# Gate products as a task of their own on DVE, full and begun output tiles in turn, small weights loaded two ahead, in a two-layer hybrid decoder trunk

## The chip, the cores and the metric

One core of one Trainium2 chip runs the whole trunk. The time is device microseconds of one execution; the median of the runs counts. TensorE (PE) makes matrix products into PSUM, VectorE (DVE), ScalarE (ACT) and GpSimd (POOL) work on tiles of 128 partitions, and SyncE (SP) issues nearly all transfers in one queue. Each engine works its queue in order.

## What is computed

Two pre-norm residual layers over 512 positions of width 2048. One input projection feeds four groups of heads (latent attention, a diagonal state-space layer, RWKV-7, differential attention) and a gate; the four outputs, concatenated, are multiplied by SiLU of the gate and projected back. Cut from the reference:

```python
def rms_norm(x, g, eps=NORM_EPS):
    xf = x.astype(jnp.float32)
    y = xf * lax.rsqrt(jnp.mean(xf * xf, axis=-1, keepdims=True) + eps)
    return (y * g.astype(jnp.float32)).astype(x.dtype)
# each layer: h = rms_norm(x); z = h @ w_in, its columns shared out among the branches;
# y = concat(mla, s5, rwkv7, diff);  x = x + (y * silu(gate)) @ w_out;  after the last layer rms_norm
```

All is float32. The weights of the large projections are 2048 x 6656 (padded) and 2048 x 2048 for each layer.

## The kernel before

All activations are kept transposed, features on partitions, as tiles of 128 x 512. Every float32 product is made of three products in a rounded format: an operand is split into a rounded high part (`wh`, `XH`, `MH`, by ACT) and the rest (`wl`, `XL`, `ML`, by DVE). `three` issues the three matmuls.

`big` is the stream that fills PE: for an output tile it walks 16 blocks of 128 inputs in pieces of four. `weights` loads a piece (`raw`, 256 KB, SP), ACT makes `wh` and DVE makes `wl`, with three buffers each (`ring`), so raw piece j waits until split j-3 is made, and the splits run up to three pieces ahead of PE. They have priority AHEAD in the compiler's scheduler, which otherwise orders ACT, DVE, POOL and SP by its own estimate of time. PE's order is written out by hand: `Clock` counts PE's time as issued products, and tasks (`spawn`) give work between two fill products when their pause, the number that they yield, is over. `late` ties an instruction behind the newest AHEAD split on its engine.

`in_proj` runs the 52 tiles of ORDER, the gate last. `evacuate` takes each tile out of PSUM on DVE; of a gate tile it makes twice SiLU in a tile `stg` (`zd` on ACT between) and, where the matching branch output is ready, goes on to `mix` at once, else stores it to DRAM (`gD`). `mix` loads the branch output `yD` into `zr`, of which there is one buffer, multiplies on POOL (L1462), and makes `MH` on ACT (L1463) and `ML` on DVE (L1464). `mix_one` fetches a stored gate tile and mixes it; `mixing` calls it at every fourth fill product.

When the first 12 gate products exist, `partial` begins output tiles over 12 of the 16 blocks, in the order of PART, and stores them as `xP`, until the other tasks are done. `out_proj` then goes through the 16 output tiles from 0 to 15: begun ones need one piece, the others four. Each is added to the residual on DVE (`xo`, L1545) and, in layer 0, given to `absorb`, which makes `XH` and `XL` of the next layer and the sum of squares (`sum_sq`: ACT squares, POOL adds, L471). The S5 tables of layer 1 (`s5_tables`) are made on DVE, ACT and POOL at the same time, with a pause of 4.5 between steps. In layer 1 `last_proj` does the same, with the final norm.

`small` does the small products of the branches (w_glu, w_uk, w_uq) with one raw buffer, the next weights loaded while one is in use.

Of the kernel before, what the change touches and what calls it, by code (L numbers as in the profile page):

```python
# [187 lines left out]
def trunk(ctx, tc, io, KT=16, depth=DEPTH):  # L188
# [45 lines left out]

    def weights(pl, src, n, bufs, first=0, into=None):

        w = WCOL
        with tc.high_priority(offset=first) if first else ExitStack():
            raw = pl.tile([128, w], F32, tag="raw", name="raw", bufs=bufs[0])
            SP.dma_start(out=raw[:, :n], in_=src)  # L240
            wh, wl = into or (pl.tile([128, w], F32R, tag=t, name=t, bufs=bufs[1]) for t in ("wh", "wl"))
            x = A.copy(out=wh[:, :n], in_=raw[:, :n])  # L242
            y = V.tensor_sub(out=wl[:, :n], in0=raw[:, :n], in1=wh[:, :n])  # L243
# [35 lines left out]
    def small(pl, srcs, nk, rh, rl, done, bufs=(1, 2)):  # L279

        nxt = weights(pl, srcs[0], nk * 128, bufs)
        for j in range(len(srcs)):
            wh, wl = nxt
            if j + 1 < len(srcs):
                nxt = weights(pl, srcs[j + 1], nk * 128, bufs)
# [53 lines left out]
    def s5_tables(pl, l, pace):  # L339
# [76 lines left out]
        for q in range(4):  # L416
# [38 lines left out]
            SP.dma_start(out=s5tab[l, q], in_=cs2.rearrange("p a g q -> p a (g q)"))  # L455


    def absorb(sp, k, x, pvt, sqs, eng=G):
# [434 lines left out]
    def s5_glu(gp, l, P, uD, ysD, out):  # L893
# [42 lines left out]
        yield from small(gp, [io["w_glu"][l, t] for t in range(4)], 4, GH, GL, done)  # L936
# [32 lines left out]
    def low_rank_col(pl, sqs, n, rxc, name, mul):  # L969
# [3 lines left out]
        yield 9.0  # L973
# [11 lines left out]
    def load_split(pl, src, n, P, g, name):  # L985
# [12 lines left out]
        for t in range(n):  # L998
# [9 lines left out]
            if t + 2 < n:  # L1008
                rs.append(load(t + 2))
                yield 4.0  # L1010
        return xh, xl, sqs

    def mla_kv(pa, l, P, aD, rxc, knD, vtD):
        def at():
            return pa.tile([128, S], F32, name="at", tag="at", bufs=3)

        kh, kl, ksq = yield from load_split(pa, aD[0:2], 2, P, "kvg", "ck")
# [9 lines left out]
        yield from small(pa, [io["w_uk"][l, h] for h in range(4)], 2, kh, kl, done)  # L1027
        ws = [weights(pa, io["w_uv"][l, :, k * 512:k * 512 + 512], 512, (1, 2)) for k in range(2)]
# [10 lines left out]
    def mla_q(pa, l, P, aD, rxc, qnD, qrD):  # L1039
        qh, ql, sqs = yield from load_split(pa, aD[3:7], 4, P, "qg", "cq")  # L1040
# [3 lines left out]
        order = (4, 5, 0, 1, 2, 3)  # L1044
# [7 lines left out]
        yield from small(pa, [io["w_uq"][l, j] for j in order], 4, qh, ql, done)  # L1052
# [258 lines left out]
    def tables(l):  # L1311
        with sub("tab", l) as st:
            yield from s5_tables(st, l, 3.0 if l == 0 else 4.5)
        PE.done.add((l, "tab"))

    class Layer:
        def __init__(self, l):
# [8 lines left out]
            self.MH, self.early, self.part, self.mixed = None, [], [], set()  # L1326
# [89 lines left out]
        def evacuate(self, n, t, ps):  # L1416
# [27 lines left out]
            else:  # L1444
# [341 lines left out]
```

## Time and profile before

| | |
|---|---|
| median of three runs | 2024.81 us (2019.72 to 2025.67) |
| the profiled execution | 2023.16 us |
| its span in the trace | 2021.4 us |
| mean granted clock of PE | 0.982 |
| PE, DVE, ACT, POOL busy | 1955.9, 1303.5, 831.8, 368.4 us |

The profile tells for each engine the time in which it was busy, what ended its idle time (the releaser), and in stretches of time what each did. PE stands at 2.4 GHz where the granted clock is 1.00 and at 1.2 GHz where it is 0.50. Matmuls are pipelined: a row's duration overlaps its neighbours', so a rate is read from the starts or from a group of them.

### The profile page before, as it was taken

What the parts mean: (1) busy time and instruction counts of PE and PEld (TensorE: products, weight loads), DVE (VectorE), ACT (ScalarE), POOL (GpSimd) and SP (SyncE); (2) the same over time, 40 slices, a digit from 0 to 9 for tenths busy, and PEclk for the clock granted to TensorE, in tenths of its full rate; (3) what the DMA queues carried; (4) which work ended last, traced back from release to release, by engine and by line L of the source; (5) the groups of instructions that cost most, each with busy time, mean ns of one, the idle gap of its engine ahead of it and who ended that gap; (6) DMA issues with size and microseconds to landing.
All of it is one profiled execution on the core that took longest, in us unless ns stands there. A gap on an engine that the chain in (4) does not pass through costs nothing.

```text
span 2021.4 us, 31452 instructions
## 1 busy us (share of the span) xinstructions
PE 1955.9 (97%) x10975; PEld 1596.9 (79%) x10975; DVE 1303.5 (64%) x2801; ACT 831.8 (41%) x1734; POOL 368.4 (18%) x422
## 2 busy tenths in 40 slices
PE   9979999999999999998999999999999998999997
PEld 7767877788888787886788888778787787887787
DVE  6886866546776577649646686664683675766442
ACT  5543434344234355434433233443332353554351
POOL 1112203123001122004101111312210112200122
PEclk9989989999999999998999999999999999999998
DMA  5453545455462455455642445365456437445553
GB/s 209 142 167 117 144 119 148 155 169 171 151 214 95 146 179 172 154 171 179 203 133 93 136 119 155 96 194 170 160 158 172 150 100 224 131 145 167 159 175 116
DMA packets 241422, 311.08 MB, mean 154 GB/s; under 512 B 83312, under 2 KB 109168, under 8 KB 241264
## 3 DMA queue, kind: packets, MB, share of 16 engines
q1 hardware_dynamic: 241120, 308.91, 49.3%
q8 instruction: 86, 1.41, 0.3%
q14 instruction: 72, 0.59, 0.1%
q10 hardware_dynamic: 144, 0.17, 0.0%
HBM read 235.75 MB, written 70.88 MB: 152 GB/s over the span
## 4 chain that ended last, share of the span: by engine, by line
PE 77%; DMA 8%; DVE 7%; ACT 3%; issue 2%; POOL 1%; SPq 1%; DVEq 0%; POOLq 0%; ACTq 0%
PE acc L126 57%; PE pb L126 18%; PE pb L130 2%; DVE wl L243 1%; DMA zr<-yD 1%; POOL stg L1462 1%; DMA raw<-in_w_out_dram 1%; DMA raw<-qkD 1%; ACT K L850 1%; DMA raw<-in_w_in_dram 1%; DMA T<-K 1%; DMA qs<-qrD 0%; SPq L854 0%; DMA xo<-xP 0%; DMA gD<-stg 0%
## 5 line engine op out<-in xcount | busy, mean ns | idle before, releaser
L126 PE MATMUL acc<-XH,wl 128*128 128x512 f32 x1600 | 654.8, 409 | 20.3 <-DVE zr L504 10.7
L126 PE MATMUL acc<-XL,wh 128*128 128x512 f32 x1600 | 629.9, 394 | 1.1 <-DVE XL L463 1.1
L126 PE MATMUL acc<-XH,wh 128*128 128x512 f32 x1600 | 629.9, 394 | 0.0
L242 ACT CAST wh<-raw 128x512 fp32r<-128x512 f32 (+1 forms) x560 | 342.4, 616 | 563.9 <-PE acc L126 415.9
L243 DVE TENSOR_TENSOR wl<-raw,wh 128x512 fp32r<-128x512 f32 (+1 forms) x560 | 395.3, 710 | 257.5 <-ACT wh L242 253.1
L126 PEld LDWEIGHTS acc<-XH,wl 128*128 128x128 f32 x1600 | 303.8, 190 | 95.2 <-DVE zr L504 11.2
L126 PEld LDWEIGHTS acc<-XH,wh 128*128 128x128 f32 x1600 | 303.1, 189 | 66.0
L126 PEld LDWEIGHTS acc<-XL,wh 128*128 128x128 f32 x1600 | 304.1, 190 | 60.7 <-DVE XL L463 2.7
L126 PE MATMUL acc<-MH,wl 128*128 128x512 f32 x448 | 180.9, 404 | 12.5 <-DVE xo L1545 10.1
L126 PE MATMUL acc<-ML,wh 128*128 128x512 f32 x448 | 176.5, 394 | 0.2 <-DVE ML L1464 0.2
L126 PE MATMUL acc<-MH,wh 128*128 128x512 f32 x448 | 176.5, 394 | 0.0
L703 POOL TENSOR_SCALAR tmp<-SV,ec 64x64 f32<-64x64 f32 x112 | 69.8, 625 | 339.8 <-DVE SV L730 171.7
L126 PEld LDWEIGHTS acc<-MH,wl 128*128 128x128 f32 x448 | 85.3, 190 | 32.7 <-DVE xo L1545 11.8
L126 PEld LDWEIGHTS acc<-MH,wh 128*128 128x128 f32 x448 | 85.0, 190 | 18.3
L126 PEld LDWEIGHTS acc<-ML,wh 128*128 128x128 f32 x448 | 85.3, 190 | 16.5 <-DVE ML L1464 0.5
L1462 POOL TENSOR_TENSOR stg<-stg,zr 128x512 f32<-128x512 f32 x32 | 45.7, 1428 | 178.3 <-DMA zr<-yD 67.4
L471 POOL TENSOR_TENSOR sqs<-sqs,sq 128x512 f32<-128x512 f32 (+1 forms) x32 | 42.3, 1321 | 133.6 <-ACT sq L469 133.5
L1279 POOL TENSOR_TENSOR sr<-ss,cc 128x1 f32<-128x1 f32 x32 | 21.8, 686 | 188.0 <-DVE ss L1277 178.2
L955 ACT ACTIVATE pt<-pb,nb,fc 128x128 f32<-128x128 f32 (+3 forms) x64 | 39.5, 618 | 32.9 <-DVE nb L954 32.5
L640 DVE TENSOR_TENSOR tmp<-X 64x30 f32<-64x30 f32 (+14 forms) x120 | 39.2, 326 | 11.0 <-DMA X<-nD 5.1
L953 DVE TENSOR_REDUCE mx<-pb 128x1 f32<-128x128 f32 (+3 forms) x96 | 45.9, 478 | 0.5
L1463 ACT ACTIVATE MH<-stg 128x512 fp32r<-128x512 f32 x32 | 20.1, 631 | 57.3 <-POOL stg L1462 50.5
(398 smaller groups left out, 2908.6 us busy)
## 6 DMA issues: line engine op xcount, KB each, us to landing
raw<-in_w_in_dram SPq DMA_DIRECT2D x416, 256.0 KB, 3.4
raw<-in_w_out_dram SPq DMA_DIRECT2D x128, 256.0 KB, 3.4
zr<-yD SPq DMA_DIRECT2D x32, 256.0 KB, 2.9
gD<-stg SPq DMA_DIRECT2D x22, 256.0 KB, 3.3
stg<-gD SPq DMA_DIRECT2D x22, 256.0 KB, 3.4
zD<-stg SPq DMA_DIRECT2D x18, 256.0 KB, 3.1
xP<-stg SPq DMA_DIRECT2D x18, 256.0 KB, 2.1
xo<-xP SPq DMA_DIRECT2D x18, 256.0 KB, 3.4
```

Of the source, the lines that this page charges most:

```text
L126: return self.nc.tensor.matmul(out, lhsT=lhsT, rhs=rhs, **kw)
L130: return self.nc.tensor.transpose(out, in_, identity)
L242: x = A.copy(out=wh[:, :n], in_=raw[:, :n])
L243: y = V.tensor_sub(out=wl[:, :n], in0=raw[:, :n], in1=wh[:, :n])
L471: eng.tensor_tensor(out=sqs, in0=sqs, in1=sq, op=ALU.add)
L640: i = V.tensor_tensor(out=t2, in0=X[:, 0:j, j:j + 1].to_broadcast([64, j, n]), in1=X[:, j:j + 1, j + 1:32].to_broadcast([64, j, n]), op=AL ...
L703: G.tensor_scalar(out=T1[T, h], in0=SVs[s][T, c, h], scalar1=ec[T, h, c:c + 1], scalar2=None, op0=ALU.mult)
L850: A.copy(out=K[:, g], in_=ps[32 * g:32 * g + 16, 0:128])
L953: V.tensor_reduce(out=mx, in_=ps[:, 0:n], axis=AX.X, op=ALU.max)
L955: A.activation(out=pt, in_=ps[:, 0:n], func=AF.Exp, scale=fcol[:, qb:qb + 1], bias=nb, accum_out=sm)
L1279: G.tensor_tensor(out=sr, in0=ss, in1=C("mhalf", 0, 1), op=ALU.pow)
L1462: G.tensor_tensor(out=g, in0=g, in1=y, op=ALU.mult)
```

## The change

A gate product is no longer made where the gate tile is. Every gate tile goes to DRAM; a task `mixer` (one for each layer, spawned with `in_proj`) takes tiles whose gate and branch output exist, loads both into one of two pairs of buffers (`zr` with `w2a2`, `y` with `lo`; the last three names are of tiles that are free by then), and a pause later issues the product on DVE, then `MH` and `ML`. `mix`, `open_mix`, `mix_one` and `mixing` are gone. `partial` stops when all 16 products exist. `out_proj` puts the begun tiles between the others. `sum_sq` adds on DVE. `weights` is cut in two, and `small` and w_uv load two pieces ahead, split with `late`. Some pauses and buffer counts are changed.

```diff
-    def small(pl, srcs, nk, rh, rl, done, bufs=(1, 2)):
-        nxt = weights(pl, srcs[0], nk * 128, bufs)
+    def small(pl, srcs, nk, rh, rl, done, raws):
+        def split(j):
+            wh, wl, x, y = split_w(pl, raws[j], nk * 128, 2)
+            late(x)
+            if j + 2 < len(srcs):
+                raws.append(load_w(pl, srcs[j + 2], nk * 128, 2))
+            return wh, wl
+        nxt = split(0)
...
-    def sum_sq(lp, sqs, src, first, eng=G):
+    def sum_sq(lp, sqs, src, first, bufs=2):
...
-            eng.tensor_tensor(out=sqs, in0=sqs, in1=sq, op=ALU.add)
+            V.tensor_tensor(out=sqs, in0=sqs, in1=sq, op=ALU.add)
...
-        yield 9.0
+        yield 6.0
...
-                yield 4.0
+                yield 3.0
...
-            t = pd.tile([128, S], F32, name="raw", tag="raw", bufs=3)
+            t = pd.tile([128, S], F32, name="raw", tag="raw", bufs=4)
...
                 r = raw(kpD)
+                load(0)
                 yield Y["ld"]
                 hd["kp"] = split("kp", r)
-                load(0)
-                yield Y["ld"]
...
-            yield from s5_tables(st, l, 3.0 if l == 0 else 4.5)
+            yield from s5_tables(st, l, 2.5 if l == 0 else 3.0)
...
-                if self.MH is not None and (l, "y", t) in PE.done:
-                    self.mix(t, g)
-                else:
-                    SP.dma_start(out=self.gD[t], in_=g)
-                    self.early.append(t)
+                SP.dma_start(out=self.gD[t], in_=g)
+                self.gates.append(t)
...
-            G.tensor_tensor(out=g, in0=g, in1=y, op=ALU.mult)
-            A.mul(out=self.MH[:, t], in_=g, mul=0.5)
...
+        def mixer(self, mctx):
+            l, on, n = self.l, [], 0
+            yield from self.need(("rwkv",))
...
+            while len(self.mixed) < 16:
+                t = next((t for t in self.gates if (l, "y", t) in PE.done), None)
+                if t is not None and len(on) < 2:
+                    self.gates.remove(t)
+                    (a, x), (b, z) = (((zp, "zr"), (cp, "w2a2")), ((mp, "y"), (cp, "lo")))[n % 2]
+                    y, g = (q.tile([128, S], F32, name=w, tag=w, bufs=1) for q, w in ((a, x), (b, z)))
+                    SP.dma_start(out=y, in_=self.yD[t])
+                    SP.dma_start(out=g, in_=self.gD[t])
+                    on.append((PE.t + Y["ld"], t, y, g))
+                    n += 1
+                elif on and on[0][0] <= PE.t:
+                    _, t, y, g = on.pop(0)
+                    late(V.tensor_tensor(out=g, in0=g, in1=y, op=ALU.mult))
+                    A.mul(out=self.MH[:, t], in_=g, mul=0.5)
...
+                yield 1.5
...
-                if (l, "others") in PE.done:
+                if len(self.mixed) == 16:
                     break
...
-            for m in range(KT):
+            order, rest = [], [m for m in range(KT) if m not in self.part]
+            for j, m in enumerate(rest):
+                order += [m] + self.part[j * len(self.part) // len(rest):(j + 1) * len(self.part) // len(rest)]
+            for m in order:
```

In SP's queue, in the gate stretch of layer 1, before (`zr` is the branch output, `stg` the gate tile, `raw<-in_w_in` a weight piece, `qkD` and `vD` the attention's tiles):

```order
L1483 DMA stg<-gD_10476 128x512
L1227 DMA raw<-qkD_10467 64x512
L1461 DMA zr<-yD_10464 128x512
L240 DMA raw<-in_w_in_dram 128x512
L1207 DMA raw<-vD_10468 128x512
L1483 DMA stg<-gD_10476 128x512
L1208 DMA raw<-qkD_10467 128x512
L1461 DMA zr<-yD_10464 128x512
L240 DMA raw<-in_w_in_dram 128x512 x2
```

and after, where the two pairs take turns:

```order
L1498 DMA w2a_17465<-gD_10493 128x512
L237 DMA raw<-in_w_in_dram 128x512 x2
L1497 DMA y<-yD_10481 128x512
L1498 DMA lo<-gD_10493 128x512
L237 DMA raw<-in_w_in_dram 128x512 x2
L1497 DMA zr<-yD_10481 128x512
L1479 DMA gD_10493<-stg 128x512
L1498 DMA w2a_17602<-gD_10493 128x512
L237 DMA raw<-in_w_in_dram 128x512 x2
```

Both loads of a product now stand together, with two weight pieces between one pair and the next.

In DVE's queue, in the same stretch, before there is `ML` alone (`pb`, `mx`, `nb` are steps of a softmax):

```order
L243 TENSOR_TENSOR wl<-raw,wh 128x512
L1449 TENSOR_TENSOR stg<-acc,rxr 128x512
L1451 SCALAR_TENSOR_TENSOR stg<-zd,stg 128x512
L243 TENSOR_TENSOR wl<-raw,wh 128x512
L1464 SCALAR_TENSOR_TENSOR ML<-stg,MH 128x512
L952 TENSOR_TENSOR pb<-pb,cc 128x128 x3
```

and after:

```order
L244 TENSOR_TENSOR wl<-raw,wh 128x512
L1503 TENSOR_TENSOR lo<-lo,y 128x512
L974 RECIPROCAL ri<-sme 128x1
L1292 TENSOR_TENSOR ri<-ri,nl 128x1
L1293 SCALAR_TENSOR_TENSOR pt<-pt,ri 128x384
L1505 SCALAR_TENSOR_TENSOR ML<-lo,MH 128x512
L1304 TENSOR_SCALAR ss<-ss 128x1
L1309 TENSOR_SCALAR on<-pb,sr 128x128
L244 TENSOR_TENSOR wl<-raw,wh 128x512
```

The product stands right behind a weight split, and its `ML` ahead of the next one.

In DVE's queue, among the output tiles of layer 0, before (`st...` and `s5par` are steps of the tables):

```order
L1545 TENSOR_TENSOR xo<-acc,xo 128x512
L410 TENSOR_SCALAR sthi<-sth 128x32
L243 TENSOR_TENSOR wl<-raw,wh 128x512
L463 SCALAR_TENSOR_TENSOR XL<-xo,pvt,XH 128x512
L310 TENSOR_SCALAR scs<-scs 128x32
```

and after:

```order
L244 TENSOR_TENSOR wl<-raw,wh 128x512
L1564 TENSOR_TENSOR xo<-acc,xo 128x512
L468 TENSOR_SCALAR cs_9814<-cs_9814,cc 128x512
L458 TENSOR_TENSOR tq<-cc,sthi 128x512
L468 TENSOR_SCALAR cs_9952<-cs_9952,cc 128x512
L244 TENSOR_TENSOR wl<-raw,wh 128x512
L458 TENSOR_TENSOR tq<-cc,sthi 128x512
L459 TENSOR_SCALAR tr<-tq 128x512
L1564 TENSOR_TENSOR xo<-acc,xo 128x512
L325 TENSOR_SCALAR cs_9814<-cs_9814 128x512
L479 SCALAR_TENSOR_TENSOR XL<-xo,pvt,XH 128x512
L459 TENSOR_SCALAR tr<-tq 128x512
L487 TENSOR_TENSOR sqs<-sqs,sq 128x512
```

The add of squares (L487) has joined each tile's work on DVE.

## Rows read from the trace of the kernel before

**Rows 1.** Page, part 1: busy us (share of the span) x instructions, each engine.
```profile
PE 1955.9 (97%) x10975; PEld 1596.9 (79%) x10975; DVE 1303.5 (64%) x2801; ACT 831.8 (41%) x1734; POOL 368.4 (18%) x422
```

**Rows 2.** Waits of PE, releaser named: us in total, times, longest.
```profile
PE acc L126 <- DVE zr L504: 10.7, 1, 10.7
PE acc L126 <- DVE xo L1545: 10.1, 4, 4.6
PE pb L126 <- ACT PT L965: 7.9, 4, 4.3
...
PE acc L126 <- DVE stg L1449: 5.2, 2, 4.9
```

**Rows 3.** Stretches: length; PE, PEld, DVE, ACT, POOL busy; clock; DMA share; GB/s.
```profile
450.00:500.00 50.00, 50.00 (x255) 40.50 (x254) 34.72 (x49) 21.67 (x38) 14.62 (x12) 1.00 0.53 174
...
750.00:800.00 50.00, 45.02 (x209) 36.72 (x208) 39.04 (x88) 26.47 (x62) 16.13 (x13) 0.93 0.56 174
```

**Rows 4.** Timeline, gate products of layer 1: SP, POOL, ACT, PE in turn.
```profile
1710.49 0.32 SPq L1461 DMA_DIRECT2D zr<-yD  x1
...
1713.45 1.75 POOL L1462 TENSOR_TENSOR stg<-stg,zr 128x512 f32<-128x512 f32 x1 [3.00 <-DMA zr<-yD]
...
1715.23 0.63 ACT L1463 ACTIVATE MH<-stg 128x512 fp32r<-128x512 f32 x1 [1.96 <-POOL stg L1462]
...
1717.37 0.80 PE L126 MATMUL acc<-XH,wl 128*128 128x512 f32 x1 [4.93 <-DVE stg L1449]
```

**Rows 5.** Chain of work, an undisturbed stretch of PE: start, us, count.
```profile
971.69 59.48 PE acc L126 x261
```

**Rows 6.** Timeline of PE: other waits of the gate stretches.
```profile
766.16 1.23 PE L126 MATMUL pb<-dVT,PT 128*128 128x128 f32 x4 [4.26 <-ACT PT L965]
...
1698.05 0.50 PE L126 MATMUL acc<-XH,wl 128*128 128x512 f32 x1 [1.57 <-DVE wl L243]
...
1912.27 0.49 PE L126 MATMUL acc<-MH,wl 128*128 128x512 f32 x1 [1.20 <-ACT MH L1463]
```

**Rows 7.** Stretches behind four waits, columns as in rows 3.
```profile
766.20:771.20 5.00, 5.00 (x16) 4.33 (x17) 4.16 (x14) 2.85 (x10) 1.30 (x2) 0.50 0.59 170
...
938.70:941.90 3.20, 3.19 (x8) 2.52 (x9) 3.20 (x8) 2.42 (x7) 1.60 (x1) 0.50 0.74 228
950.60:954.60 4.00, 4.00 (x10) 3.13 (x11) 4.00 (x9) 2.43 (x4) 2.59 (x2) 0.50 0.99 334
1717.40:1723.40 6.00, 6.00 (x14) 4.75 (x15) 3.32 (x6) 2.60 (x5) 2.46 (x2) 0.50 0.50 144
```

**Rows 8.** Page, parts 5 and 6: groups (busy, mean ns) and transfers (us to landing).
```profile
L242 ACT CAST wh<-raw 128x512 fp32r<-128x512 f32 (+1 forms) x560 | 342.4, 616 | 563.9 <-PE acc L126 415.9
...
L1462 POOL TENSOR_TENSOR stg<-stg,zr 128x512 f32<-128x512 f32 x32 | 45.7, 1428 | 178.3 <-DMA zr<-yD 67.4
...
zr<-yD SPq DMA_DIRECT2D x32, 256.0 KB, 2.9
```

**Rows 9.** Groups on DVE by line, 0 to 40 us.
```profile
L463 DVE SCALAR_TENSOR_TENSOR XL<-x,pvt,XH 128x512 fp32r<-128x512 f32 x16 | 11.6, 750 | 0.6 <-ACT XH L462 0.6
L471 DVE TENSOR_TENSOR sqs<-sqs,sq 128x512 f32<-128x512 f32 x15 | 10.3, 690 | 0.4
```

**Rows 10.** Output tiles of layer 0: two stretches, then groups of 903 to 1028 us.
```profile
903.00:1028.00 125.00, 113.65 (x478) 91.81 (x477) 87.33 (x191) 55.70 (x105) 37.62 (x28) 0.96 0.58 183
923.00:983.00 60.00, 48.65 (x192) 37.94 (x191) 58.77 (x138) 28.75 (x59) 18.16 (x11) 0.91 0.60 186
...
L243 DVE TENSOR_TENSOR wl<-raw,wh 128x512 fp32r<-128x512 f32 x40 | 27.9, 699 | 25.5 <-ACT wh L242 25.5
L463 DVE SCALAR_TENSOR_TENSOR XL<-xo,pvt,XH 128x512 fp32r<-128x512 f32 x16 | 17.0, 1061 | 0.7
L1545 DVE TENSOR_TENSOR xo<-acc,xo 128x512 f32<-128x512 f32 x16 | 11.0, 685 | 9.3 <-PE acc L126 7.1 <-DMA xo<-xP 2.2
```

**Rows 11.** Timeline of ACT: a cast of keys in layer 1.
```profile
1840.12 0.62 ACT L1240 CAST dk<-raw 128x512 fp32r<-128x512 f32 x1 [4.11 <-DMA raw<-qkD]
```

More of the change, by code (lines that the diff above doesn't have):

```diff
@@ L232, in trunk, with load_w, split_w @@
     s5b = dram("s5b", [depth, 4, 128, 2, 2, 64])
-    def weights(pl, src, n, bufs, first=0, into=None):
[L237 to L243, printed above, removed]
+    def load_w(pl, src, n, bufs):
+        raw = pl.tile([128, WCOL], F32, tag="raw", name="raw", bufs=bufs)
+        SP.dma_start(out=raw[:, :n], in_=src)
+        return raw
+    def split_w(pl, raw, n, bufs, into=None):
+        wh, wl = into or (pl.tile([128, WCOL], F32R, tag=t, name=t, bufs=bufs) for t in ("wh", "wl"))
+        x = A.copy(out=wh[:, :n], in_=raw[:, :n])
+        y = V.tensor_sub(out=wl[:, :n], in0=raw[:, :n], in1=wh[:, :n])
+        return wh, wl, x, y
+    def weights(pl, src, n, bufs, first=0, into=None):
+        with tc.high_priority(offset=first):
+            raw = load_w(pl, src, n, bufs[0])
+            wh, wl, x, y = split_w(pl, raw, n, bufs[1], into)
             if first == AHEAD:
@@ L284, in small @@
             if j + 1 < len(srcs):
-                nxt = weights(pl, srcs[j + 1], nk * 128, bufs)
+                nxt = split(j + 1)
             yield Y["small0"] if j == 0 else Y["small"]
@@ L454, in s5_tables, with absorb @@
                             op0=ALU.mult, op1=ALU.mult)
-            SP.dma_start(out=s5tab[l, q], in_=cs2.rearrange("p a g q -> p a (g q)"))
-    def absorb(sp, k, x, pvt, sqs, eng=G):
+            yield pace
+            late(SP.dma_start(out=s5tab[l, q], in_=cs2.rearrange("p a g q -> p a (g q)")))
+    def absorb(sp, k, x, pvt, sqs, first):
         g = pvt[:, PV["norm_g"][0] + k:PV["norm_g"][0] + k + 1]
@@ L905, in load @@
             return u, y
+        srcs = [io["w_glu"][l, t] for t in range(4)]
         nxt = load(0)
+        raws = [load_w(gp, x, 512, 2) for x in srcs[:2]]
         for t in range(4):
@@ L934, in done @@
             out(4 + t, o)
-        yield from small(gp, [io["w_glu"][l, t] for t in range(4)], 4, GH, GL, done)
+        yield from small(gp, srcs, 4, GH, GL, done, raws)
     def softmax(pl, ps, qb, fcol, fneg, tag, bufs):
@@ L1025, in done @@
             SP.dma_start(out=knD[h], in_=t)
-        yield from small(pa, [io["w_uk"][l, h] for h in range(4)], 2, kh, kl, done)
-        ws = [weights(pa, io["w_uv"][l, :, k * 512:k * 512 + 512], 512, (1, 2)) for k in range(2)]
+        yield from small(pa, srcs, 2, kh, kl, done, raws)
+        raws = [load_w(pa, io["w_uv"][l, :, k * 512:k * 512 + 512], 512, 2) for k in range(2)]
+        yield 7.0
+        ws = []
+        for k in range(2):
+            wh, wl, x, y = split_w(pa, raws[k], 512, 2)
+            late(x)
+            ws.append((wh, wl))
         for t in range(4):
@@ L1039, in mla_q @@
     def mla_q(pa, l, P, aD, rxc, qnD, qrD):
+        order = (4, 5, 0, 1, 2, 3)
+        srcs = [io["w_uq"][l, j] for j in order]
+        raws = [load_w(pa, x, 512, 2) for x in srcs[:2]]
         qh, ql, sqs = yield from load_split(pa, aD[3:7], 4, P, "qg", "cq")
@@ L1050, in done @@
             SP.dma_start(out=qnD[j] if j < 4 else qrD[j - 4], in_=o)
-        yield from small(pa, [io["w_uq"][l, j] for j in order], 4, qh, ql, done)
+        yield from small(pa, srcs, 4, qh, ql, done, raws)
         return qc, qn
@@ L1669, in everything @@
             with ExitStack() as mctx:
-                yield from L.in_proj(mctx, begun)
+                PE.spawn(L.mixer(mctx), 2)
+                yield from L.in_proj(begun)
                 begun = []
-                yield from L.partial(mctx)
-                while L.early or (l, "others") not in PE.done:
-                    if not L.mix_one(mctx):
-                        yield False
+                yield from L.partial()
+                while len(L.mixed) < 16:
+                    yield False
                 with sub("wp", l) as wp:
```

58 lines of the change are left out of this document (19 added, 39 removed).

## Prediction

> **What bounds the kernel now.** I read the share of busy time first: PE is busy 97% of the 2021.4 us span, DVE 64%, ACT 41%, POOL 18% [rows 1]. The work of PE does not change: both kernels issue the same 6720 matrix products of the projections and the same small ones. So the change can win only what PE idles, and what it then runs at the lower level of its clock. The second view, what PE waited for, names the idle time: one wait of 10.7 us for `zr`, 10.1 us in four waits for `xo`, 7.9 us in four for `PT`, 5.2 us in two for the gate tile `stg` [rows 2]. The third view, stretches of time, tells full ones (450 to 500 us) from those with idle time, as 750 to 800 us, where PE is busy 45.02 of 50 us [rows 3]; the others are the gate products of layer 1, the output tiles of layer 0, the start and the end. The last two are no part of this: up to about 400 us the order of PE is the same row by row in both kernels, so the `zr` wait stays, and the end (2000 us on) keeps its chain of sum, power, scale and store.
>
> **Gate products (the first large term).** At 1707 to 1717 us the rows show one product after the other [rows 4]. SP can issue the load of `zr` only when the product before has read that one buffer; POOL then waits for the load (3.00 us), multiplies in 1.75 us, and ACT's copy `MH`, which comes before the next weight cast `wh` in ACT's queue, waits for POOL 1.96 us. One round takes 4.7 us, from the issue at 1710.49 to the end of the product at 1715.20. PE consumes a weight piece (12 products) in 2.73 us, from 59.48 us for 261 products in an undisturbed stretch [rows 5]. So ACT falls behind PE while the products run, and PE then idles 4.93 us for the gate tile that DVE could not take. The same stands at 766.16 us (4.26 us for `PT`, a copy that stood behind `MH` on ACT), at 1698.05 us (1.57 us) and at 1912.27 us (1.20 us) [rows 6]. Together 4.93 + 4.26 + 1.57 + 1.20 = 12.0 us. After the two long ones the granted clock is 0.50, which is 1.2 GHz, for at least 5.0 and 6.0 us [rows 7]; half of each is lost, 2.5 + 3.0 = 5.5 us. **The term is 17.5 us.**
>
> What replaces it: two sets of two buffers, both loads issued ahead, and the product on DVE at a place of its own. A raw weight piece j waits for split j-3, so by the new order I count, for each of the 32 products, the pieces between the later of its two loads and the product itself: 21 have four pieces or more (10.9 us), two have three, eight have two (5.5 us) and one has one (2.7 us). Landing takes 2.9 us [rows 8]. No row of before shows this wait on DVE; by these numbers it is nothing but for one product, about 1 us, and the lead of three pieces in front of PE covers that. I take nothing. The product itself: 1428 ns on POOL [rows 8], on DVE some 0.69 us by the nearest DVE row, the sum-of-squares add of the start of the program with the same shape [rows 9]. It adds 32 x 0.69 = 22 us to DVE. Against that stands what POOL's work takes from DVE: `XL` averages 1061 ns where POOL adds squares beside it and 750 ns where it adds nothing [rows 9, 10], and the product on POOL goes with the same kind of row. DVE gets fuller by between 0.69 - 0.31 = 0.38 and 0.69 us per product; nine in 50 us add 3 to 6 us, from 78% in 750 to 800 us [rows 3] to between 84 and 90%, and its queue has a lead of three pieces (8.2 us) on PE. I price this and everything else that is new in the order at 3 us, about what the `PT` waits other than the longest make together today (7.9 - 4.26 = 3.6 us in three) [rows 2, 6]; the bounds are 0 and 22 us (every product on the path).
>
> The Trainium skill (Perfetto Trace Analysis, Optimizing Scalar/DVE Operations) speaks against this step: where DVE is saturated, work should go from it to ScalarE or even GpSimd, though it adds that the two share a read port so that it may not help. By that rule the next term would be lost; that result is the first rival below.
>
> **Output tiles of layer 0 (the second term).** In 923 to 983 us PE is busy 48.65 of 60 us, so it idles 11.35 us, and DVE is busy 58.77 [rows 10]. There DVE is the bound: it makes the tables of the next layer, the weight splits, and for every output tile an add (0.69 us), `XL` and nothing else, while a begun tile keeps PE for one piece of 2.73 us only. The old order has three begun tiles in a row twice. After two of the waits the clock is 0.50 for 3.2 and 4.0 us [rows 7], 3.6 us lost. **The term is 11.35 + 3.6 = 15.0 us.**
>
> The new order puts full and begun tiles in turn (nine begun tiles, never more than two in a row). It also gives DVE the add of squares, 0.69 us for each tile, and takes the same add from POOL; `XL` should fall from 1061 to 750 ns, which it has where POOL adds nothing [rows 9, 10]. So a tile costs DVE 0.69 + 0.75 + 0.69 = 2.13 us in place of 1.75. All of 903 to 1028 us holds 87.33 us of DVE, of which splits, `XL` and adds are 27.9 + 17.0 + 11.0 [rows 10]; the tables are the other 31.4 us. By the order they now lie within 25 weight pieces, 68.3 us of PE, with 11 tiles. DVE then has 31.4 + 25 x 0.70 + 11 x 2.13 = 72.3 us to do in 68.3 us of PE: short by 4 us, of which that lead can hide all or nothing. I keep 3 us of stall and clock, with bounds 0 and 8 us. **The gain is 12 us.** POOL's sums of squares in the last projection run where DVE has room; there and at the end I take nothing.
>
> **Edits that I cost at nothing.** Small weights two ahead, their loads before the norms, shorter pauses (9.0 to 6.0, 4.0 to 3.0), tables at another pace, the earlier first load and a fourth `raw` buffer in the attention: they move pieces of 410 to 540 us, 1400 to 1540 us and 1580 to 1660 us by 2 to 10 us on PE. PE stands there at 50.00 of 50 us [rows 3], so the cover is PE's own work, and what a slip would cost is in the 3 us. The pace of the tables of layer 0 changes no row of the order before 240 us. The smaller `PT` waits, 3.6 us, stay too: before the longest of them ACT stands 4.11 us for a load of keys [rows 11], and those loads keep their distance from their casts in the new order (two pieces).
>
> **The sum.** The profiled execution took 2023.16 us; it lies 1.65 below the median, within the 6 us that the three runs spread. 2023.2 - 17.5 - 12 + 3 = 1996.7, so **1997 us**. A measurement of this kernel can tell about 0.3%, 6 us, from no change. Best case: both terms whole, and the smaller `PT` waits won too: 2023.2 - 17.5 - 15.0 - 3.6 = 1987.1. Worst case of the same mechanism: 8 us kept in the output tiles and 8 us of new waits, 2023.2 - 17.5 - 7 + 8 = 2007.
>
> **Rivals.**
> First, DVE becomes the bound in the output tiles. For: it is at 98% there now [rows 10], and 15 adds come to it. Against: the tiles alternate, and POOL leaves it alone. Then nothing of the 15 us is won and 8 us of new waits come: 2023.2 - 17.5 + 8 = 2014.
>
> Second, the waits only change place. Against it: the chain in [rows 4] is named link by link. For it: ACT still waits for keys [rows 11], and three stages have a new order. New waits eat the gain: 2021.
>
> Third, slower: ACT and DVE take turns. In the new order of ACT's queue `MH` stands before the next `wh`, and waits for a product that stands on DVE behind a split and softmax steps; the next split then waits for that `wh`. POOL no longer works beside them. If `MH` (0.63 us) and `wh` (616 ns) [rows 4, 8] are each time exposed on DVE, that is 1.25 us for each of 32 products, 40 us, and the gate term is not won: 2023.2 - 12 + 40 = 2051; with half of the products so, 2031. It decides when DVE has no slack left within the two pieces (5.5 us) from product to product. Against it: DVE is busy 78% and ACT 53% in 750 to 800 us [rows 3].
>
> **How the numbers follow.** Forecast 0.70, DVE as bound 0.13, waits that move 0.08, turns of ACT and DVE 0.09. Faster by over 0.3% are the first two, 0.83; within it 0.08; slower 0.09. The range goes from 1985 (best case and the spread of runs) to 2015, which takes in the first rival and leaves out the other two.
>
> **What would show it.** Right: at the gate stretches no wait of PE over 1 us with release by `MH`, `PT` or the gate tile, and ACT's idle before `MH` small; PE waits for `xo` in the output tiles of layer 0 under 4 us with DVE still near full; `XL` near 0.75 us; clock 1.00 in 750 to 800 and 1700 to 1750. The 10.7 us at 100 us and the end unchanged. Wrong: DVE products with long idle time for `gD` or `yD`; PE waits for `wl` in the gate stretches; or new waits of PE in the small products.

## The result and the profile after

The changed kernel takes 1999.47 us in the median (1995.7 to 2002.24), the kernel before 2022.26 us in the runs taken with it. The ratio of the changed kernel to the one before, taken in the same set of runs, is 0.9888, with a 95% interval from 0.9862 to 0.9914: 22.8 us less. The forecast was 1997 us with a range from 1985 to 2015, so the time lies in the range, 2.5 us above the forecast. A later set of runs gave 0.9888 again, with an interval from 0.9872 to 0.9905. All ratios below are to the kernel before in the same set, with their 95% intervals in brackets. Each trace is of one execution, which can lie some us off the median of its kernel.

The profiled execution of the changed kernel has a span of 2000.5 us; that of before had 2021.4 us. Its busy times, in the form of [rows 1]:

```profile
PE 1947.6 (97%) x10975; PEld 1591.5 (80%) x10975; DVE 1320.2 (66%) x2866; ACT 833.7 (42%) x1734; POOL 278.5 (14%) x358
```

DVE has 17 us more, POOL 90 us less. The waits of PE, in the form of [rows 2]:

```profile
PE acc L126 <- DVE zr L520: 10.7, 1, 10.7
PE acc L126 <- DVE wl L244: 5.5, 6, 1.9
PE acc L126 <- DVE xo L1581: 4.3, 2, 3.2
PE pb L130 <- DVE pt L1293: 3.7, 2, 2.4
PE pb L126 <- ACT PT L983: 3.4, 4, 1.5
...
PE acc L126 <- DVE xo L1564: 1.4, 2, 1.0
```

The gate tile `stg` and the copy `MH` no longer stand here. `xo` of layer 0 (L1564) is down from 10.1 us to 1.4 us and `PT` from 7.9 us to 3.4 us. Two entries have grown from next to nothing: `xo` of the last projection (L1581) has 4.3 us, which was 0.2 us before, and `pt` (L1293), a step of a softmax, has 3.7 us. The two gate stretches, in the columns of [rows 3]; the first answers its second row:

```profile
750.00:800.00 50.00, 50.00 (x245) 41.78 (x244) 43.01 (x106) 30.90 (x70) 2.16 (x4) 1.00 0.73 230
1700.00:1750.00 50.00, 48.67 (x243) 40.73 (x242) 40.40 (x105) 30.75 (x75) 3.27 (x6) 1.00 0.63 200
```

PE is full in the first, at a granted clock of 1.00, which is 2.4 GHz; before, it was busy 45.02 of 50 us at 0.93. DVE went from 39.04 to 43.01 us there, 86%, inside the 84 to 90% that were forecast.

**Where the time came from.** Both kernels issue 6720 products of the projections, with the same number in each stage, so the start of the n-th one can be set side by side. The numbers below are starts in the two traces, taken at points where the same small products are done.

| product | before | after | difference | what lies between |
|---|---|---|---|---|
| 1200 | 399.8 | 399.6 | -0.2 | start, identical order |
| 2880 | 922.2 | 921.8 | -0.4 | attention and gates of layer 0 |
| 3240 | 1020.8 | 1005.5 | -15.3 | output tiles of layer 0 |
| 4440 | 1372.3 | 1357.0 | -15.3 | the first half of layer 1 |
| 6120 | 1908.9 | 1882.6 | -26.2 | attention and gates of layer 1 |
| 6240 | 1938.1 | 1916.1 | -22.0 | start of the last projection |
| 6716 | 2007.1 | 1986.1 | -21.0 | the rest |

The output tiles won 15 us and layer 1 won 11 us. Two places show nothing like what was forecast: layer 0 won nothing before its output tiles, though its gate stretch is full now, and the last projection gave 4 us back.

### The profile page after: what moved, and what is told of

It reads as the page before. It is cut to its first block, busy times and chain, and to the rows that moved or that the text cites. A ratio compares the mean times of both kernels' runs of the same rounds, so it can differ in the third digit from the quotient of the medians.

```text
span 2000.5 us, 31433 instructions
## 1 busy us (share of the span) xinstructions
PE 1947.6 (97%) x10975; PEld 1591.5 (80%) x10975; DVE 1320.2 (66%) x2866; ACT 833.7 (42%) x1734; POOL 278.5 (14%) x358
## 4 chain that ended last, share of the span: by engine, by line
PE 46%; DMA 3%; DVE 3%; ACT 1%; issue 1%; POOL 0%; SPq 0%; DVEq 0%; ACTq 0%
PE acc L126 37%; PE pb L126 8%; PE pb L130 1%; DMA raw<-in_w_out_dram 1%; DMA raw<-qkD 1%; DMA raw<-in_w_in_dram 1%; DVE wl L244 1%; ACT K L866 0%; DMA xo<-xP 0%; DMA U<-uD 0%; POOL smag L367 0%; DMA tmp<-bvD 0%; DMA NM<-zD 0%; DVE Fo L1615 0%; DMA qkD<-rt 0%
## 5 line engine op out<-in xcount | busy, mean ns | idle before, releaser
L243 ACT CAST wh<-raw 128x512 fp32r<-128x512 f32 x560 | 342.1, 616 | 573.7 <-PE acc L126 449.0
L244 DVE TENSOR_TENSOR wl<-raw,wh 128x512 fp32r<-128x512 f32 x560 | 390.8, 702 | 239.9 <-ACT wh L243 237.5
L126 PEld LDWEIGHTS acc<-XH,wl 128*128 128x128 f32 x1600 | 301.9, 189 | 89.6 <-DVE zr L520 11.2
L970 DVE TENSOR_TENSOR pb<-pb,cc 128x128 f32<-128x128 f32 x96 | 26.3, 295 | 28.1 <-PE pb L126 26.6
L660 DVE TENSOR_TENSOR X<-X,tmp 64x30 f32<-64x30 f32 (+14 forms) x120 | 38.5, 321 | 2.6
L746 DVE SCALAR_TENSOR_TENSOR SV<-pb,ec,tmp 64x64 f32<-64x64 f32 x96 | 27.1, 283 | 19.5 <-PE pb L126 17.0
```

The lines of the kernel that those rows point to most:

```text
L126: return self.nc.tensor.matmul(out, lhsT=lhsT, rhs=rhs, **kw)
L660: V.tensor_tensor(out=X[:, 0:j, j + 1:32], in0=X[:, 0:j, j + 1:32], in1=t2, op=ALU.add)
L746: V.scalar_tensor_tensor(out=SVs[s][T, c + 1, h], in0=po[h][T, 64:128], scalar=ec[T, h, c:c + 1], in1=T1[T, h], op0=ALU.mult, op1=ALU.add)
L970: V.tensor_tensor(out=ps[:, qb * 128:n], in0=ps[:, qb * 128:n], in1=C("neg"), op=ALU.add)
```

## Experiments on the output tiles

**Tiles in the old order**, squares still on DVE:

```
-            for m in order:
+            for m in range(KT):
```

> The changed kernel (1999.5 us), but the output tiles of layer 0 go from 0 to 15 again; sums of squares stay on DVE. Theory, the turns of full and begun tiles carry the 15 us that the output tiles of layer 0 gained: DVE falls behind in the runs of begun tiles, PE waits 8 to 12 us for xo there and drops to a clock of 0.5 after, time 2010 to 2014. Rival, the gain comes from the squares and the tables (POOL no longer beside DVE, tables at a smaller pause): PE waits under 3 us for xo and the time stays within 1999 to 2003.

Measured: 2007.65 us, ratio 0.9935 (0.9918 to 0.9952), between the two theories.

**Squares on POOL**, tiles in turn:

```
-            V.tensor_tensor(out=sqs, in0=sqs, in1=sq, op=ALU.add)
+            eng.tensor_tensor(out=sqs, in0=sqs, in1=sq, op=ALU.add)   # POOL, DVE at the start
```

> The changed kernel, but the sums of squares of the output tiles are added on POOL as before (those at the start stay on DVE). Theory, the turns alone suffice: XL goes back to about 1.06 us, DVE has 0.68 us less for the add and 0.32 us more for XL per tile, PE waits for xo stay under 3 us, time 1998 to 2001. Rival, the freed DVE (no POOL add beside it) is needed: PE waits 4 us or more for xo in layer 0 and the time is 2004 to 2010.

Measured: 2000.85 us, ratio 0.9903 (0.9888 to 0.9918). The theory held, with `XL` at 905 ns and not quite back at 1.06 us.

**Both undone:**

> The changed kernel with both edits of the output tiles undone: tiles from 0 to 15, squares on POOL. Undone alone they cost 7 us and 1 us in that stretch of the changed kernel; the whole gain there was 15 us. Theory, the edits replace each other (squares on DVE matter only where begun tiles stand in a row): 12 to 15 us lost in that stretch, ratio 0.995 to 0.997. Rival, the rest of the gain comes from the tables at a smaller pause and from POOL's products gone: 7 to 9 us lost, ratio 0.992 to 0.994.

Measured: 2013.14 us, ratio 0.9957 (0.9943 to 0.9972). The theory held.

**The kernel before with the tiles in turn** and nothing else:

> The kernel before with one edit, full and begun output tiles of layer 0 in turn; sums of squares on POOL, tables at the old pace. Theory, the turns give half of the 15 us (going back to the old order alone cost the changed kernel 7 us in that stretch): 2012 to 2015 with PE waiting 3 to 5 us for xo. Rival, the turns alone suffice: 2005 to 2008 with under 2 us of waits; other rival, without the faster tables nothing is won: 2018 to 2022.

Measured: 2009.58 us, ratio 0.9960 (0.9947 to 0.9973). That is some 8 us won, by the order of the tiles alone, between the first two expectations.

The stretch from 905 to 975 us shows all of them, in the columns of [rows 3]. Here is its row in the kernel before:

```profile
905.00:975.00 70.00, 58.65 (x235) 46.21 (x234) 61.65 (x152) 33.45 (x67) 29.48 (x19) 0.93 0.61 192
```

in the changed kernel with both edits undone:

```profile
905.00:975.00 70.00, 61.30 (x246) 48.65 (x246) 63.09 (x157) 35.04 (x71) 26.93 (x15) 0.93 0.59 189
```

with the tiles in the old order alone:

```profile
905.00:975.00 70.00, 62.81 (x270) 49.78 (x269) 63.36 (x168) 38.34 (x76) 12.23 (x8) 1.00 0.64 209
```

with the squares on POOL alone:

```profile
905.00:975.00 70.00, 66.39 (x286) 52.67 (x285) 62.66 (x157) 34.94 (x72) 26.07 (x14) 1.00 0.62 202
```

and in the changed kernel:

```profile
905.00:975.00 70.00, 68.11 (x296) 54.85 (x295) 62.45 (x168) 36.24 (x73) 11.29 (x7) 1.00 0.63 201
```

Read the second number of each (PE busy) with the one in brackets behind it (its products). PE waits for `xo` of layer 0 for 11.2 us in all with both undone, 7.1 in the old order, 2.4 with squares on POOL and 1.4 in the changed kernel. DVE is busy 62 to 63 us of 70 in the four versions of the changed kernel: it is near full in each, and what differs is how its work meets PE's. From the start of product 2820 to that of 3300 the changed kernel takes 113.0 us, 115.7 with the squares on POOL, 118.9 in the old order, 127.0 with both undone, and the kernel before takes 126.7. So the two edits make the whole gain of this stretch; the tables at a smaller pause and all else that stays when both are undone (nine tiles begun ahead in layer 0, where the kernel before begins eight) make none of it. In these traces they are not a sum: the order is worth 11.3 us with squares on POOL and 5.9 us with squares on DVE; the squares 8.1 us in the old order and 2.7 us in the new one. The times do not show this. By the ratios, of 2020 us, both together are worth 13.9 us, the order 10.9 and 9.5 us and the squares 4.4 and 3.0 us, each with an uncertainty of 4 to 6 us, and the traced execution of the old order alone was the fastest of its four, 2002.84 us against a median of 2007.65 us. So the order is the larger part, what the squares add is small, and whether both remove the same waits stays open.

How squares on DVE can help an engine that is near full is in the groups of 890 to 1030 us (columns as in [rows 10]). Both versions have the old order. With squares on POOL:

```profile
L244 DVE TENSOR_TENSOR wl<-raw,wh 128x512 fp32r<-128x512 f32 x45 | 33.0, 734 | 24.5 <-ACT wh L243 24.4
L479 DVE SCALAR_TENSOR_TENSOR XL<-xo,pvt,XH 128x512 fp32r<-128x512 f32 x16 | 15.0, 938 | 0.7 <-ACT XH L478 0.2
L460 DVE TENSOR_TENSOR tq<-tq,tr 128x512 f32<-128x512 f32 x4 | 3.8, 953 | 0.0
```

and with squares on DVE:

```profile
L244 DVE TENSOR_TENSOR wl<-raw,wh 128x512 fp32r<-128x512 f32 x48 | 32.8, 684 | 22.7 <-ACT wh L243 22.7
L479 DVE SCALAR_TENSOR_TENSOR XL<-xo,pvt,XH 128x512 fp32r<-128x512 f32 x16 | 11.8, 738 | 0.5
L487 DVE TENSOR_TENSOR sqs<-sqs,sq 128x512 f32<-128x512 f32 x15 | 10.2, 677 | 0.0
L460 DVE TENSOR_TENSOR tq<-tq,tr 128x512 f32<-128x512 f32 x4 | 2.6, 673 | 0.0
```

Beside POOL's adds (1700 ns each) many of DVE's groups are slower. These three alone lose 45 x 0.050 + 16 x 0.200 + 4 x 0.280 = 6.6 us; the remaining groups of the tables bring it to about 10 us, which is what the 15 adds cost on DVE itself. The add `xo`, which takes one operand out of PSUM, hardly changes (685 against 679 ns). So the adds come to DVE for nothing. Why that wins time, 8 us in this pair of traces and 4.4 us by the ratios, is argued, not shown: the add has no priority and goes where DVE has room, while POOL's slowed whatever stood beside it, the splits that PE waited for among them.

## Experiments on the gate products

**The product on POOL**, the task otherwise as it is:

```
-                    late(V.tensor_tensor(out=g, in0=g, in1=y, op=ALU.mult))
+                    G.tensor_tensor(out=g, in0=g, in1=y, op=ALU.mult)
```

> The changed kernel, but the gate product of the new task runs on POOL (about 1.43 us instead of 0.685). Theory, the task of its own with two pairs of buffers and both loads ahead is what removed the waits: no wait of PE over 2 us in the gate stretches (740 to 830 us, 1670 to 1810 us), time 1998 to 2002. Rival, the engine is what counts: ACT waits longer for MH in front of the next weight cast, PE waits 5 to 10 us more there with its clock at 0.5 behind, time 2006 to 2012.

Measured: 2023.13 us, ratio 1.0011 (1.0001 to 1.0021). The whole gain of the change is gone, and the time is slower than either expectation, so at first sight the engine decides. But the edit also takes away `late`, the tie that holds the product behind the newest weight split. Counted in the order of the queues, `MH` then stands up to three weight pieces nearer to the loads of its operands. ACT's `MH` in this version, then in the changed kernel:

```profile
L1504 ACT ACTIVATE MH<-lo 128x512 fp32r<-128x512 f32 x16 | 10.1, 632 | 31.0 <-POOL lo L1503 31.0
L1504 ACT ACTIVATE MH<-w2a 128x512 fp32r<-128x512 f32 x16 | 10.1, 631 | 32.6 <-POOL w2a L1503 25.3 <-DMA yD<-tmp 7.3
```

```profile
L1504 ACT ACTIVATE MH<-lo 128x512 fp32r<-128x512 f32 x16 | 10.1, 634 | 12.6 <-DVE lo L1503 12.6
L1504 ACT ACTIVATE MH<-w2a 128x512 fp32r<-128x512 f32 x16 | 10.1, 633 | 19.6 <-DVE w2a L1503 18.3 <-DVE mx L971 1.4
```

ACT idles 63.6 us before its 32 copies; in the changed kernel 32.2 us. Three more versions part engine and place.

**POOL, with `MH` tied** behind the newest weight cast:

```
-                    A.mul(out=self.MH[:, t], in_=g, mul=0.5)
+                    late(A.mul(out=self.MH[:, t], in_=g, mul=0.5))
```

> The changed kernel with the product on POOL again, but ACT's copy MH tied behind the newest weight cast, so that MH stands as many weight pieces behind its loads as in the changed kernel (with the product on POOL and no tie it stood up to three pieces nearer, and the time was 2023.1 us). Theory, the place counts: MH finds its operands loaded, ACT does not stand before the casts, time 2000 to 2005. Rival, the engine counts: POOL's 1.4 us beside a slowed DVE keeps MH late, PE waits 6 us or more in the gate stretches, time 2010 to 2023.

Measured: 2022.56 us, ratio 1.0022 (1.0013 to 1.0032). By its numbers the rival won, but the trace names another cause. ACT's idle time before `MH` is down to 25 us; now DVE waits. The group of `on` on DVE in this version, then in the changed kernel:

```profile
L1309 DVE TENSOR_SCALAR on<-pb,sr 128x128 f32<-128x128 f32 x32 | 11.1, 348 | 35.3 <-POOL sr L1306 33.3 <-POOL zr L518 2.0
```

```profile
L1309 DVE TENSOR_SCALAR on<-pb,sr 128x128 f32<-128x128 f32 x32 | 11.1, 347 | 9.5 <-POOL sr L1306 9.1 <-PE pb L130 0.4
```

and one case in time order, POOL first:

```profile
1730.18 1.26 POOL L1503 TENSOR_TENSOR lo<-lo,y 128x512 f32<-128x512 f32 x1 [4.62 <-issue]
1731.40 1.06 POOL L1306 TENSOR_TENSOR sr<-ss,cc 128x1 f32<-128x1 f32 x2
...
1731.99 0.35 DVE L1309 TENSOR_SCALAR on<-pb,sr 128x128 f32<-128x128 f32 x1 [5.32 <-POOL sr L1306]
```

The untied product stands early in POOL's queue and waits there for its load (the row names no releaser, but the load of `lo` was issued at 1725.92 us and landed at 1730.06 us); `sr`, a tile of one column that DVE needs at once, stands behind it, and DVE stands 5.32 us. In the changed kernel DVE waits 9.1 us for `sr` in the whole program, here 33.3 us.

**POOL, product and `MH` both tied** behind the newest split and cast:

```
+                    for m in PE.mark.values():
+                        tc.add_manual_dep(x.ins, m.name, ...)   # x is the product on POOL
```

> The changed kernel with the product on POOL and everything that follows the DVE product's place kept: product and MH both tied behind the newest weight split and cast. In the run before, only MH was tied; the product then stood early in POOL's queue, waited there for its load, and DVE waited 33 us (9 us in the changed kernel) for the small sr behind it. Theory, the place in every queue is what counts and the engine little: DVE's wait for sr goes back to about 10 us, no wait of PE over 2 us in the gate stretches, ratio to the kernel before 0.989 to 0.992, some 2000 to 2006 us. Rival, the engine counts by itself (1.4 us instead of 0.69, DVE slowed beside it): waits of 6 us or more stay, ratio 0.995 to 1.002.

Measured: 2004.37 us, ratio 0.9914 (0.9898 to 0.9930). The theory held but for one wait of 2.33 us at 1765 us, which begins at a product that POOL starts late. DVE's group of `on` is back near its old idle time:

```profile
L1309 DVE TENSOR_SCALAR on<-pb,sr 128x128 f32<-128x128 f32 x32 | 11.2, 349 | 14.1 <-POOL sr L1306 11.9 <-POOL zr L518 2.1
```

and the gate stretch of layer 0 is full, with the product on POOL (busy 14.10 us, the fifth busy time, against 2.16 us in the changed kernel):

```profile
750.00:800.00 50.00, 50.00 (x244) 41.58 (x243) 43.28 (x104) 30.64 (x71) 14.10 (x13) 1.00 0.75 237
```

**DVE, without the tie:**

```
-                    late(V.tensor_tensor(out=g, in0=g, in1=y, op=ALU.mult))
+                    V.tensor_tensor(out=g, in0=g, in1=y, op=ALU.mult)
```

> The changed kernel with the product on DVE but without the tie behind the newest weight split, so that products and MH stand one to four weight pieces nearer to their loads. Theory, the place counts: ACT and now DVE wait for gD and yD in front of casts and splits, PE waits over 8 us more in the gate stretches, time 2012 to 2025. Rival, the engine counts: the time stays at 1999 to 2003.

Measured: 2032.89 us, ratio 1.0082 (1.0063 to 1.0101), slower than the kernel before and slower than expected. The products on DVE in this version:

```profile
L1503 DVE TENSOR_TENSOR w2a<-w2a,zr 128x512 f32<-128x512 f32 x16 | 11.1, 692 | 24.0 <-DMA w2a<-gD 17.6 <-DMA zr<-yD 6.4
L1503 DVE TENSOR_TENSOR lo<-lo,y 128x512 f32<-128x512 f32 x16 | 11.1, 691 | 23.9 <-DMA lo<-gD 12.8 <-DMA y<-yD 11.0
```

with the longest wait of PE:

```profile
788.64 0.66 PE L130 MATMUL pb<-cc,pt 128*128 128x128 f32 x2 [7.88 <-DVE pt L1293]
```

and in the changed kernel:

```profile
L1503 DVE TENSOR_TENSOR w2a<-w2a,zr 128x512 f32<-128x512 f32 x16 | 11.0, 686 | 3.0 <-DMA w2a<-gD 1.6 <-DMA zr<-yD 1.4
L1503 DVE TENSOR_TENSOR lo<-lo,y 128x512 f32<-128x512 f32 x16 | 11.0, 686 | 1.3 <-DMA y<-yD 1.3
```

Without the tie DVE stands 47.9 us for loads in front of its products, with it 4.3 us; the softmax steps behind it come late and PE waits once for 7.88 us. So the gate term rests first on the place. By the ratios to the kernel before, which took about 2020 us in each set of runs, the tie is worth (1.0082 - 0.9888) x 2020 = 39 us for the product on DVE; on POOL, tying the product as well as `MH` is worth (1.0022 - 0.9914) x 2020 = 22 us; and with the place right, DVE in the stead of POOL is worth 2004.37 - 1999.59 = 4.8 us on the same chip, where the two intervals just overlap. All these versions have the two pairs of buffers; what they are worth against the single buffer of before was not measured by itself.

## Experiments on the new waits

**Attention begun as before:**

```
-            t = pd.tile([128, S], F32, name="raw", tag="raw", bufs=4)
+            t = pd.tile([128, S], F32, name="raw", tag="raw", bufs=3)
...
-                load(0)
                 yield Y["ld"]
                 hd["kp"] = split("kp", r)
+                load(0)
+                yield Y["ld"]
```

> The changed kernel, but latent attention starts as before (three raw buffers, the first head's loads one pause later). Theory, the earlier start makes the new waits of PE near 579 to 622 us (0.67, 0.39, 1.47, 0.43, 0.43, 0.31 us, and a clock of 0.97 in 600 to 650 us): the key casts stand in ACT's queue ahead of weight casts and wait for their loads; with the old start these waits go and the time is 1994 to 1997. Rival, they come from the shorter pauses or the weights loaded ahead: the waits stay, time 1999 to 2001.

Measured: 1997.76 us, ratio 0.9891 (0.9876 to 0.9905), no difference from the changed kernel's 0.9888. The waits went as the theory has it, and the gain in time did not come. In the changed kernel the latent attention of layer 0 begins earlier, and casts of its keys stand in ACT's queue ahead of weight casts and wait for their loads. ACT, then PE, in time order:

```profile
574.89 0.62 ACT L1118 CAST kph<-raw 128x512 fp32r<-128x512 f32 x1 [2.95 <-DMA raw<-kpD]
...
596.17 0.49 PE L126 MATMUL pb<-PT,VT 128*128 128x128 f32 x2 [1.47 <-ACT PT L983]
...
734.50 0.55 PE L130 MATMUL pb<-cc,pt 128*128 128x128 f32 x3 [2.38 <-DVE pt L1293]
```

Its stretch from 575 to 740 us:

```profile
575.00:740.00 165.00, 158.50 (x1129) 127.42 (x1128) 102.59 (x269) 70.58 (x171) 20.48 (x32) 0.99 0.42 136
```

With the old start the stretch is full (first row), and another wait comes in the next attention, where ACT again stands 3.42 us for keys (ACT, then PE):

```profile
575.00:740.00 165.00, 164.97 (x1172) 133.87 (x1170) 106.51 (x276) 71.70 (x171) 16.83 (x29) 1.00 0.46 150
```

```profile
835.63 0.62 ACT L1268 CAST dk<-raw 128x512 fp32r<-128x512 f32 x1 [3.42 <-DMA raw<-qkD]
...
836.68 1.65 PE L126 MATMUL pb<-dVT,PT 128*128 128x128 f32 x6 [3.45 <-ACT PT L983]
```

From product 1200 to product 2880 this version takes 518.2 us, the changed kernel 522.2 us; by product 4440 the 4 us are lost again, with a wait of 1.99 us for `XH` at 1012 us among the causes. The edit also moves more than it names: ten and eleven tiles are begun ahead in the two layers in place of nine and ten, PE waits 2.51 us for `wl` at 1695 us, and the wait at 1891 us of the next experiment is absent. So the earlier start makes the waits of 575 to 740 us, and its worth for the whole program is not isolated.

**Output tile 0 begun first**, so that it is not the last to be stored:

```
-PART = (1, 2, 5, 6, 9, 10, 3, 7, 11, 0, 4, 8)
+PART = (0, 1, 2, 5, 6, 9, 10, 3, 7, 11, 4, 8)
```

> The changed kernel with output tile 0 begun first instead of tenth. Theory, the last projection's first tile waits for the load of a partial result that was stored right before (store issued at 1883.6 us, load at 1888.0, add at 1890.7, PE waits 3.18 us and then runs 7 us at a clock of 0.5): with tile 0 stored long before, the wait at 1891 us and the slow stretch go, 3 to 5 us less than the changed kernel, 1995 to 1997. Rival, the buffers of the last projection come free too late anyway: the wait stays and the time too, 1999 to 2000.

Measured: 1994.81 us, ratio 0.9887 (0.9872 to 0.9903). The wait is gone in the trace, but the kernel before ran at 2017.9 us in this set, so the ratio shows no gain over 0.9888. Both then ran on one chip:

> The changed kernel itself, on the chip of these runs, for comparison with the next: ratio 0.987 to 0.991, and in the last projection a wait of 1.5 to 3.2 us for xo with a slow stretch behind it.

> Output tile 0 begun first, against the changed kernel on the same chip. Theory: 3 to 6 us faster than it, by the wait for xo, its slow stretch and the 1.1 us at the first half tile (1957 us of the changed kernel) that are gone in the trace. Rival: within 2 us, since the trace of the changed kernel was taken in an execution with a long wait.

Measured: the changed kernel 1999.59 us (1996.28 to 2001.26), ratio 0.9888 (0.9872 to 0.9905); tile 0 first 1992.96 us (1991.79 to 1993.53), ratio 0.9857 (0.9842 to 0.9872). No run of the one reaches those of the other: 6.6 us on this chip. The ratio of the first set was 0.9887, so the times alone give between nothing and 6.6 us. The traces say where it lies: from product 6120 to 6716 the two of the changed kernel take 103.5 and 99.7 us, the two with tile 0 first 95.9 and 96.6 us, 3 to 8 us less in the last projection. The new trace of the changed kernel missed its expectation: the wait was 1.37 us, with no slow stretch behind it. In the first trace of the changed kernel (SP, DVE, PE):

```profile
1883.55 0.33 SPq L1526 DMA_DIRECT2D xP<-stg  x1
...
1887.96 0.80 SPq L1591 DMA_DIRECT2D xo<-xP  x2
...
1890.66 1.36 DVE L1581 TENSOR_TENSOR xo<-acc,xo 128x512 f32<-128x512 f32 x2 [3.77 <-DMA xo<-xP]
...
1891.41 0.80 PE L126 MATMUL acc<-MH,wl 128*128 128x512 f32 x1 [3.18 <-DVE xo L1581]
```

Then what SP waited for between 1880 and 1895 us, and the stretch:

```profile
SPq L1591 <- DMA xP<-stg: 3.4, 1, 3.4
```

```profile
1890.00:1898.00 8.00, 6.59 (x17) 5.22 (x18) 3.02 (x5) 2.99 (x5) 0.00 (x0) 0.57 0.47 160
```

The first tile of the last projection reads back what was stored last: 4.41 us from store to load, of which SP stands 3.4 us for the store to land, 2.7 us more to the add, and PE waits for its accumulator, then runs at a clock that averages 0.57. With tile 0 begun first, both loads go out before the last two stores, and PE is full:

```profile
1867.02 0.88 SPq L1591 DMA_DIRECT2D xo<-xP  x2
```

```profile
1870.00:1900.00 30.00, 30.00 (x134) 24.84 (x133) 14.33 (x21) 11.86 (x20) 0.00 (x0) 1.00 0.56 183
```

It is the fastest version of this study.

## Why the prediction was right, and where it was not

**Gate products (17.5 us forecast).** The waits of 4.26, 4.93 and 1.20 us [rows 4, 6] are gone, with the two slow stretches behind the first two: 10.4 us of idle time and 5.5 us of clock. The fourth was put down wrongly: the 1.57 us at 1698 us came when ACT stood in front of an `MH` for the store of the branch's output, and in the changed kernel a wait of 1.58 us stands at nearly the same place of the program (product 5340, before 5364), now behind a step of DVE that waits for `bvD`. First ACT before, then DVE and PE after:

```profile
1694.71 1.16 ACT L1463 ACTIVATE MH<-stg 128x512 fp32r<-128x512 f32 x2 [5.79 <-DMA yD<-tmp]
```

```profile
1672.38 0.75 DVE L780 SCALAR_TENSOR_TENSOR tmp<-pb,pvt,tmp 128x512 f32<-128x512 f32 x1 [5.08 <-DMA tmp<-bvD]
...
1673.79 0.50 PE L126 MATMUL acc<-XH,wl 128*128 128x512 f32 x1 [1.58 <-DVE wl L244]
```

The product on DVE measured 686 ns against 0.69 us, and its loads cost DVE 4.3 us in all. At most one wait of PE, 0.63 us at 1682.89 us, stands behind them, and there DVE had also stood 0.75 us for a cast of keys: the count of pieces between load and product was the right thing to look at. What the text did not see is how much hangs on it. It named the engine, the single buffer and the round of 4.7 us as the cause; the runs show that, with two pairs of buffers, the place in the queues of ACT, DVE and POOL carries 22 us and more, the engine 5 us, and they leave the single buffer open. Its signs came in part: ACT's idle time before `MH` fell from 57.3 to 32.2 us only, and in layer 1 PE still has waits over 1 us, 1.58 us for `wl`, 1.33 us for `pt` (at 1705 us) and 1.17 us for `PT` (at 1803 us).

**The rival in which ACT and DVE take turns** (2031 to 2051 us) did not come. The version without the tie comes to its time, 2032.9 us, and to its sign, ACT idle for 59 us before `MH`, but not by its mechanism: there DVE stands 47.9 us for loads, which the rival does not name, so the same number is no proof of it. What that version shows is that the term hangs on the tie, one line in the diff. The prediction gave DVE's busy share, 78% in 750 to 800 us, as the reason against turns. Without the tie that share is 76% (the third busy time), and PE is busy 40.22 us only, so the share does not tell a safe order from a slow one:

```profile
750.00:800.00 50.00, 40.22 (x182) 32.80 (x181) 38.00 (x97) 25.64 (x58) 1.63 (x3) 0.90 0.65 212
```

**Output tiles (15 us, of which 12 forecast).** The whole came, 14.9 us. DVE is near full there, as forecast, `XL` fell to 743 ns against the 0.75 us named, and the 4 us by which DVE seemed short were hidden but for 1.4 us of waits for `xo`. The term was undersized by 3 us. The step that left something out is the price of the add: the text let it cost DVE 0.38 us for each tile, with `XL` alone faster, while the groups above show that much of DVE's other work gets faster too, and that the adds cost DVE nothing in sum. That the 3 us come from this step is not shown; the squares in the new order are worth 2.7 us in the traces.

The Trainium skill (Perfetto Trace Analysis, Optimizing Scalar/DVE Operations) says that offloading some work from a saturated DVE to ScalarE or even GpSimd may make sense, and in the same place that between DVE and GpSimd, which share an SBUF read port, it might not help. Here the traces bear the warning out: `XL` takes 905 to 1061 ns beside POOL's adds and 743 ns without them. The times lean the same way but are not apart: squares on POOL gave 0.9903 and squares on DVE 0.9888 in the new order, 0.9957 and 0.9935 in the old one, with intervals that overlap. The Trainium skill (SBUF — State Buffer, Who interferes with whom) says that a DVE instruction with two SBUF inputs contends with a GpSimd instruction that reads SBUF; `XL` and POOL's add have these forms.

**The edits at nothing and the 3 us for small waits** are where it was off. The earlier attention made waits of 0.67, 0.39, 1.47, 0.43, 0.31, 0.85 and 2.38 us in 579 to 735 us, 6.5 us; they ate what layer 0 won at its gates. With the old start these are gone, though that edit moved other things as well. The text priced every small wait together by three `PT` waits of before and never looked at what the earlier casts queue behind on ACT. The last projection's 4 us was missed for a plainer reason: the text took nothing there and took no account of the store that its first load must follow. In the kernel before, PE waited 1.20 us for `MH` at that place, which may have covered part of it; no run shows this.

**The sum** holds because misses cancel. In the two traces the gains are 15.9 us at the gates (17.5 forecast), 14.9 us in the output tiles (12 forecast) and some 5 us that were not forecast: the `tmp` wait of 2.1 us near 1563 us with 1.8 us of clock behind it, and 1.2 us of the `PT` wait at 1841 us. Against them stand about 15 us of new waits with their clock, of which 3 were forecast: 6.5 us in layer 0, 2 us at the gates of layer 1 (1.33 and 0.63 us), 5.4 us in the last projection (4.2, and the 1.2 us that stood there before as the `MH` wait), 1 us elsewhere. Waits well under 1 us, and the clock of 0.99 in 575 to 740 us, are left out, so the account closes to some 2 us and no better. The rival in which the waits only change place was thus half true: more came back than the 3 us allowed, but not the gain. That leaves 21 us in this pair of executions, where the forecast had 26.5; the medians are 22.8 us apart. Why the `tmp` wait went was not isolated: it stayed away with the old attention start too, so it is not that edit. Nor was any run made with the small weights one ahead or the old pauses alone; what those edits are worth is not shown.

## What to carry to other kernels

When an operation moves to another engine, fix its place in every in-order queue that it and its followers stand in, and count the pieces between load and use; a product at the wrong place cost 22 us and more here, on the slower engine 5 us. Where one engine is the bound for a stretch, mix long and short pieces of the other engine's work before making anything faster: here that was worth 8 us by itself. A read of what has just been written back should not be the first thing of a stage.

## What the runs showed that was not expected

A wait on POOL for a 256 KB load was paid by DVE through a tile of one column that stood behind it: 33.3 us of DVE's time in place of 9.1 us. A partial result stored and read back at once took 4.4 us from the issue of the store to the issue of the load in one trace of the changed kernel and let PE wait 3.18 us, with a clock of 0.57 behind; in the other trace of the same kernel it took 2.3 us, the wait was 1.37 us and the clock stayed at 1.00. From product 6120 to 6240 the same program thus took 33.5 and 29.8 us.
